# A hybrid attention / mLSTM / Hyena backbone: the late adaLN modulation computed by row sums on VectorE instead of matmuls

## The chip, the core and the metric

The kernel runs on one core of one Trainium2 chip. The metric is the device time of one execution in microseconds (us). The median of three runs of the kernel before is 3824.61 us (3822.61 to 3828.31).

## The reference, cut to what matters

Two layers (`DEPTH = 2`) work on 1024 latent tokens and 256 context tokens of width 1024. Each layer normalises its tokens, projects them, runs three groups of mixers side by side (latent attention with 8 heads, a chunked mLSTM, a Hyena convolution), projects back, and ends with a ConvFFN. Everything is modulated by six vectors per layer and stream:

```
for i in range(DEPTH):
    mod_x = jax.nn.silu(c) @ ada_w[i] + ada_b[i]        # ada_w[i]: 1024 x 6144
    mod_c = jax.nn.silu(c_ctx) @ ada_w[i] + ada_b[i]
    sh1, sc1, g1, sh2, sc2, g2 = jnp.split(mod_x[:, None, :], 6, axis=-1)
    csh1, csc1, cg1, csh2, csc2, cg2 = jnp.split(mod_c, 6, axis=-1)
    hx = rmsnorm(x, norm1_g[i]) * (1.0 + sc1) + sh1
    ...
    x = x + g1 * (jnp.concatenate([att_x, ml_x, hy_x], axis=-1) @ w_out[i])
    x = x + g2 * conv_ffn(rmsnorm(x, norm2_g[i]) * (1.0 + sc2) + sh2, ...)
```

So each of the two streams (latent and context) needs 6144 dot products of length 1024 per layer; in layer 1 the context stream needs only `csh1` and `csc1`, because its output is not used. The values depend on nothing but `c`, `c_ctx` and weights. `sh1` and `sc1` are needed at the start of a layer, `g1` at its output projection, `sh2` and `sc2` at its second norm, `g2` at the end of its FFN.

## The kernel before, in words

Features lie on the 128 partitions, tokens along the columns, in blocks of 512, 512 and 256 (context) columns. A float32 product is carried by three float32r matmuls (`mm3`) of hi and lo parts; a weight tile is loaded into `wr`, cast to hi on ScalarE (line 300) and its lo part is a subtraction on VectorE, or on GpSimd during the FFN (line 301).

The stages of a layer follow each other, layer 0 and then layer 1, and overlap at their ends:

- **mixers** (`mixers_in`): input projections on TensorE; `conv_tiles` makes a depthwise convolution along a row `raw` with one ScalarE and two VectorE instructions; `ml_states` and `ml_out` are the mLSTM, in which each chunk of 128 tokens makes a small tile `nd` on VectorE;
- **hyena** (`hyena`);
- **attention** (`attention`): units of one block of queries and one head. A unit of a latent block has ten steps, one per tile of 128 keys: three matmuls into a bank `st` (96 or 97 rows x 512), two exponentials on ScalarE (`P` and its rounded form `Ph`), `Pl = P - Ph` on VectorE in even steps and on GpSimd in odd steps (line 1344), three matmuls into `pv`. Between the steps, row maxima of the coming unit are taken: one matmul into a bank `sm` (two banks) and a VectorE reduction (line 1308). Layer 0 has 16 such units and 8 short ones for context queries; layer 1 has the 16 alone;
- **w_out** and the second norm, then **ffn**: 44 products (`begin`, `piece`) into one of two PSUM tiles `u3` of 1536 columns in layer 0, each followed by `conv` (one ScalarE and two VectorE passes over the tile), interleaved with the down projection in two banks `pj` and `pk`, whose results VectorE adds to the stream (line 1515).

The modulation is made by `ada`: four loads of 256 KB of `ada_w`, 8 matmuls with the 32-column stationary `cs` (silu of both conditions; the profile shows each of them as two), a ScalarE copy of the bank into `adarow`, 2 small matmuls that fold it, a VectorE addition into `mods`. One call makes 256 features of both streams. The first 8 calls (`sh1`, `sc1` of layer 0) run at the start. The other 40, that is 16 for layer 0 and 24 for layer 1, all run in the attention of layer 0, six after each pair of units, planned as if traced 300 instructions later (`after`, `LATER_A`); they use the bank `pk` and five blocks `ada_w` of the ring `B`.

The order on every engine is not written by hand: a planner (`schedule_with_timeline_sim=True`) simulates the program with its own costs and issues what is ready by priority, which is the order of tracing. Once planned it is fixed: each engine and each DMA queue works through its list in order and waits at the head of it. Nearly all loads are issued by one queue, SyncE's (SP).

Of the kernel before, what the change touches and what calls it, by code (L numbers as in the profile page):

```python
# [9 lines left out]
F32 = mybir.dt.float32  # L10
# [12 lines left out]
TP = 1282                     # token axis with a zero after each stream: x 0:1024, 0, ctx 1025:1281, 0  # L23
# [11 lines left out]
# (first token, columns, stream: 0 latent / 1 context)  # L35
# [16 lines left out]
def _consts():  # L52
# [47 lines left out]
def _host(inp):  # L100
    """Lay the inputs out for the chip: slices, transposes, replication."""
# [4 lines left out]
    def colmaj(a):                       # [L, n*128] -> [L, 128, n]  # L106
        return a.reshape(a.shape[0], -1, 128).transpose(0, 2, 1)
# [3 lines left out]
    o["adaw"] = g["ada_w"].reshape(L, 4, 2, 128, 12, 512).transpose(0, 4, 1, 3, 2, 5).reshape(L, 12, 4, 128, 1024)  # L111
# [48 lines left out]
    qk = np.zeros((L, 2, 2, 128, 128), np.float32)           # [L, pair, q/k, in, out]  # L160
# [9 lines left out]
    o["hyv"] = np.stack([g["hy_b1"], g["hy_b2"], g["hy_sin_freq"]], -1)   # [L,64,3]  # L170
# [12 lines left out]
NADA = 6  # L183
# [6 lines left out]
class Kern:  # L190
    def __init__(self, tc, a, out):
        self.tc, self.nc, self.a, self.out = tc, tc.nc, a, out
        self.n = self.turn = self.wturn = 0
        self.wx = None
# [48 lines left out]
    def later(self, by):  # L243
        """Scheduled as if traced `by` instructions later: work that fills gaps."""
# [9 lines left out]
    def mm3(self, out, lh, ll, rh, rl, start, stop):  # L254
        """One K tile of a float32 product carried by three float32r passes."""
# [1187 lines left out]
    def ffn(self, L, xs, hs, rp, pp, between):  # L1443
# [19 lines left out]
        def conv(u):  # L1463
# [6 lines left out]
            if ab == 0:  # L1470
                nc.scalar.activation(y[:, :W], y[:, :W], AF.Silu)
# [217 lines left out]
```

## Time and profile before

| | |
|---|---|
| median of three runs | 3824.61 us (3822.61 to 3828.31) |
| profiled execution: span from first to last instruction | 3828.4 us (no other time of it is given; the highest of the three runs is 3828.31) |
| TensorE matmul (PE) busy | 3547.6 us (93%), 17696 instructions |
| VectorE (DVE) busy | 2001.4 us (52%), 3037 instructions |
| ScalarE (ACT) busy | 1294.6 us (34%) |
| GpSimd (POOL) busy | 923.9 us (24%) |
| HBM read | 263.50 MB |

Busy time of PE is a model for overlapping matmuls: a busy PE need not run at its peak. PEld is its weight load, which overlaps. [...] SPq is the queue of SyncE, which issues DMAs. Stages by the trace: mixers of layer 0 from about 95 to 400 us, attention of layer 0 from about 584 (its first exponential) to 1046 us (the first result of the output projection), FFN of layer 0 to about 2100; mixers of layer 1 from about 2200 to 2489 and its attention from 2629 (table load of its exponentials) to 2976.

### The profile page before, as it was taken

To read this page: it belongs to the slowest core of one execution; us is meant where nothing else is said; L and a number is where in the kernel's file an instruction comes from. 1 tells how busy PE (TensorE), PEld (TensorE's weight loads), DVE (VectorE), ACT (ScalarE), POOL (GpSimd) and SP (SyncE) were. 2 spreads that over 40 slices of the span, in tenths; PEclk is the share of its full clock that TensorE was granted. 3 is DMA by queue.
4 is the path that set the end of the run, shared out by engine and by line. 5 is a ranking of instruction groups with operands and counts; after the bars stand their busy time and mean duration, and the time that the engine had idled before them with its cause. 6 is when DMAs were issued, how large, how long until landed. Compare 5 with 4: busy or idle time off the path is not lost.

```text
span 3828.4 us, 45926 instructions
## 1 busy us (share of the span) xinstructions
PE 3547.6 (93%) x17696; PEld 2809.5 (73%) x17696; DVE 2001.4 (52%) x3037; ACT 1294.6 (34%) x2108; POOL 923.9 (24%) x782
## 2 busy tenths in 40 slices
PE   5999869989899999999999799978999999999997
PEld 3798755556677888888888678856666778888885
DVE  5646675445565433434334765566666543444345
ACT  4433314445543221212112443324566432222222
POOL 1402442222311111111112141143334122222221
PEclk8999989989999999999999899889999999999998
DMA  5322544466242111111111222343232311111111
GB/s 176 115 69 90 198 130 141 126 168 170 71 138 66 39 34 39 39 33 34 39 39 39 94 95 88 108 141 105 54 84 80 102 44 44 45 55 45 44 50 66
DMA packets 195007, 319.46 MB, mean 83 GB/s; under 512 B 32207, under 2 KB 112160, under 8 KB 194788
## 3 DMA queue, kind: packets, MB, share of 16 engines
q1 hardware_dynamic: 194244, 316.23, 26.6%
q8 instruction: 139, 2.28, 0.3%
q14 instruction: 80, 0.66, 0.1%
q0 software_dynamic: 544, 0.31, 0.0%
HBM read 263.50 MB, written 52.81 MB: 83 GB/s over the span
## 4 chain that ended last, share of the span: by engine, by line
PE 59%; DVE 6%; DMA 3%; ACT 2%; issue 2%; POOL 1%; SPq 0%; DVEq 0%; ACTq 0%; POOLq 0%
PE u L252 29%; PE pk L252 12%; PE pj L252 12%; PE st L252 2%; PE pv L252 2%; PE hf L252 1%; ACT wh L300 1%; PE mi L252 0%; DVE B L456 0%; DMA vst<-Ph 0%; PE sm L252 0%; DVE sa L453 0%; PE mo L252 0%; DMA B<-mix 0%; DVE S L1515 0%
## 5 line engine op out<-in xcount | busy, mean ns | idle before, releaser
L252 PE MATMUL u<-B,wh 128*128 128x512 f32 (+1 forms) x3240 | 727.0, 376 | 17.6 <-ACT wh L300 10.6
L252 PEld LDWEIGHTS u<-B,wh 128*128 128x128 f32 x3240 | 573.9, 189 | 141.3 <-ACT wh L300 12.7
L301 POOL TENSOR_TENSOR wh<-wr,wh 128x1024 fp32r<-128x1024 f32 x92 | 222.3, 2416 | 1116.1 <-ACT wh L300 1116.1
L300 ACT CAST wh<-wr 128x1024 fp32r<-128x1024 f32 (+2 forms) x188 | 188.8, 1005 | 775.9 <-PE u L252 425.8
L252 PE MATMUL u<-B,wx 128*128 128x512 f32 (+1 forms) x2040 | 435.1, 367 | 2.3 <-DVE sa L1469 2.3
L252 PEld LDWEIGHTS u<-B,wx 128*128 128x128 f32 x2040 | 352.6, 189 | 70.9 <-issue 2.5
L252 PE MATMUL pj<-B,wh 128*128 128x512 f32 (+1 forms) x1644 | 381.8, 378 | 16.2 <-DVE wh L301 7.0
L252 PE MATMUL pk<-B,wh 128*128 128x512 f32 (+1 forms) x1485 | 355.9, 386 | 31.9 <-ACT S L588 7.8
L252 PEld LDWEIGHTS pj<-B,wh 128*128 128x128 f32 x1644 | 288.5, 193 | 83.6 <-issue 11.9
L252 PEld LDWEIGHTS pk<-B,wh 128*128 128x128 f32 x1485 | 265.7, 197 | 102.2 <-issue 15.3
L1515 DVE SCALAR_TENSOR_TENSOR S<-pk,mods,S 128x512 f32<-128x512 f32 (+1 forms) x220 | 152.7, 694 | 322.5 <-PE pk L252 322.3
L1344 POOL TENSOR_TENSOR Pl<-P,Ph 128x512 fp32r<-128x512 f32 (+1 forms) x168 | 219.4, 1306 | 405.9 <-ACT Ph L1343 349.1
L1515 DVE SCALAR_TENSOR_TENSOR S<-pj,mods,S 128x512 f32<-128x512 f32 (+1 forms) x220 | 152.7, 694 | 307.9 <-PE pj L252 307.8
L252 PE MATMUL st<-qh,S 96*128 96x512 f32 (+1 forms) x960 | 292.7, 411 | 15.1 <-DMA qh<-mr 7.9
L1308 DVE TENSOR_REDUCE mx<-sm 128x1 f32<-128x512 f32 (+1 forms) x400 | 227.6, 588 | 116.4 <-PE sm L252 114.1
L1468 DVE SCALAR_TENSOR_TENSOR sa<-u,ffc,sa 128x1281 f32<-128x1281 f32 (+1 forms) x88 | 124.3, 1413 | 276.3 <-ACT sa L1467 275.0
L1342 ACT ACTIVATE P<-st 128x512 f32<-128x512 f32 (+1 forms) x336 | 197.9, 590 | 162.0 <-PE st L252 82.4
L252 PE MATMUL pk<-g,wh 128*128 128x512 f32 (+1 forms) x1032 | 242.2, 370 | 7.7 <-ACT g L283 3.6
L252 PE MATMUL pj<-g,wh 128*128 128x512 f32 (+1 forms) x1032 | 245.1, 370 | 2.7 <-POOL wh L301 1.6
L252 PEld LDWEIGHTS st<-qh,S 96*128 96x128 f32 (+1 forms) x960 | 183.0, 196 | 75.0 <-DMA qh<-mr 12.2
L252 PE MATMUL pv<-Ph,B 128*64 128x512 f32 (+2 forms) x672 | 213.1, 398 | 12.7 <-ACT Ph L1343 8.4
L252 PEld LDWEIGHTS pk<-g,wh 128*128 128x128 f32 x1032 | 179.6, 189 | 43.8 <-DVE S L1515 4.2
(391 smaller groups left out, 5048.5 us busy)
## 6 DMA issues: line engine op xcount, KB each, us to landing
B<-in_adaw_dram SPq DMA_DIRECT2D x192, 256.0 KB
wr<-in_wup_dram SPq DMA_DIRECT2D x88, 512.0 KB
wr<-in_wdn_dram SPq DMA_DIRECT2D x50, 512.0 KB
wr<-in_wout_dram SPq DMA_DIRECT2D x40, 512.0 KB
wr<-in_win_dram SPq DMA_DIRECT2D x28, 512.0 KB
S<-in_xT_dram SPq DMA_DIRECT2D x16, 640.0 KB
mlrb<-rrows SPq DMA_DIRECT2D x36, 256.0 KB
B<-mix SPq DMA_DIRECT2D x32, 256.0 KB
```

Of the source, the lines that this page charges most:

```text
L252: self.nc.tensor.matmul(out, lhsT, rhs, start=start, stop=stop)
L300: self.nc.scalar.copy(hi, wr)
L301: (self.nc.gpsimd if self.wpool else self.nc.vector).tensor_tensor(lo, wr, hi, op=ALU.subtract)
L1308: nc.vector.reduce_max(st["mx"][:, qt, bi:bi + 1], ps[:, :kn], axis=AX.X)
L1342: nc.scalar.activation(P[:, :n], ps[:, :n], AF.Exp, scale=SCALE)
L1344: (nc.gpsimd if j % 2 else nc.vector).tensor_tensor(Pl[:, :n], P[:, :n], Ph[:, :n], op=ALU.subtract)
L1468: nc.vector.scalar_tensor_tensor(y[:, 1:W], pu[:, 0:W - 1], cw[:, 0:1], y[:, 1:W], op0=ALU.mult, op1=ALU.add)
L1515: nc.vector.scalar_tensor_tensor(x, ps, self.mods[L][:, 40 + m, s:s + 1], x, op0=ALU.mult, op1=ALU.add)
```

## The change

The 8 calls of `ada` at the start stay. The other 40 go, and the same features are made by VectorE alone. The host lays the rest of `ada_w` out transposed (`adawT`: 80 tiles of 128 features x 1024). Silu of both conditions is also made as two rows and kept in DRAM (`silu_rows`, `crow`); a stage loads pieces of them, repeated on all 128 partitions (`crows`). One `tensor_tensor_reduce` multiplies a piece of a weight tile (256 or 512 columns) by the row, sums along the columns, adds the bias or the sum so far, and writes one column of `mods`. It also has to write its products somewhere: they go over a tile that the stage has just finished with (`out`), which ties the instruction to its place.

`ada_rows` is a generator that issues the loads and the sums; a stage starts it (`ada_start`) and sends it such tiles (`ada_some(out, n)`: n sums). Where they are: after each convolution of the mixers (4, over `raw`) and each mLSTM chunk (4, over `nd`); in attention after the even steps of a unit (1, over `P`, in step 4 two); in the FFN of layer 0 after each convolution (3, over the PSUM tile `u3`).

| stage | features | columns | sums | loads, KB each |
|---|---|---|---|---|
| mixers 0 | 16 to 23 of layer 0, both streams | 256 | 64 | 32 x 128 |
| attention 0 | 24 to 47 of layer 0, both streams | 512 | 96 | 48 x 256 |
| FFN 0 | 0 to 15 of layer 1, both streams | 256 | 128 | 64 x 128 |
| mixers 1 | 16 to 31 of layer 1, latent | 256 | 64 | 64 x 128 |
| attention 1 | 32 to 47 of layer 1, latent | 512 | 32 | 32 x 256 |

(A feature here is a group of 128.) The counts follow from the calls below: groups x pieces of a row of 1024 x streams. The pool of `P` in attention goes from two buffers to three, in both layers; the weight tiles have their own buffers (`aw`: 3 or 4 in the mixers, 2 in attention, 3 in the FFN). The diff also removes comments, which are left out here.

```
...
+    def silu_rows(self, sp):
+        nc = self.nc
+        r = self.t(sp, [2, 1024], "crow")
+        nc.sync.dma_start(r, self.a["cb"])
+        nc.scalar.activation(r, r, AF.Silu)
+        nc.sync.dma_start(self.crow[:, :], r)
+
+    def crows(self, t, s, c0):
+        n = t.shape[-1]
+        self.nc.sync.dma_start(t, self.crow[s, c0:c0 + n].unsqueeze(0).to_broadcast([128, n]))
+        return t
+
+    def ada_rows(self, L, fs, streams, n, wt, rt):
+        nc = self.nc
+        for c0 in range(0, 1024, n):
+            rows = [(s, self.crows(rt(s, c0), s, c0)) for s in streams]
+            for f in fs:
+                w = wt()
+                nc.sync.dma_start(w, self.a["adawT"][f - 16 if L == 0 else 32 + f][:, c0:c0 + n])
+                for s, r in rows:
+                    out = yield
+                    m = self.mods[L][:, f, s:s + 1]
+                    nc.vector.tensor_tensor_reduce(out=out[:, :n], in0=w, in1=r, scale=1.0,
+                                                   scalar=m if c0 else self.adab[L][:, f, s:s + 1],
+                                                   op0=ALU.mult, op1=ALU.add, accum_out=m)
+
+    def ada_some(self, out, n=1):
+        try:
+            for _ in range(n):
+                if self.adas is not None:
+                    self.adas.send(out)
+        except StopIteration:
+            self.adas = None
...
+            self.ada_some(raw, 4)
             ys.append(y)
...
+            rm = self.pool(e, f"rm{L}", aw=4 if last else 3)
+            self.ada_start(L, range(16, 32) if last else range(16, 24), (0,) if last else (0, 1), 256,
+                           lambda: self.t(rm, [128, 256], "aw"),
+                           lambda s, c0: self.t(rm, [128, 256], f"ar{s}"))
...
+                self.ada_some(nd.rearrange("p a b c -> p (a b c)"), 4)
                 nc.gpsimd.tensor_tensor(hh[:, 0], hh[:, 0], hh[:, 1], op=ALU.add)
...
                 (nc.gpsimd if j % 2 else nc.vector).tensor_tensor(Pl[:, :n], P[:, :n], Ph[:, :n], op=ALU.subtract)
+                if j % 2 == 0:
+                    self.ada_some(P, 2 if j == 4 else 1)
...
-                after()
...
             nc.vector.scalar_tensor_tensor(y[:, 0:W - 1], pu[:, 1:W], cw[:, 2:3], y[:, 0:W - 1], op0=ALU.mult, op1=ALU.add)
+            self.ada_some(pu, 3)
...
+                self.silu_rows(rp)
                 for nb in range(4):
                     for half in range(2):
                         self.ada(0, nb, half, lambda: self.blk(dt=F32), pp, "a0")
...
-                todo = [(x, i, h) for x, a0 in ((0, 4), (1, 0)) for i in range(a0, 12) for h in range(2)] if L == 0 else []
-
-                def next_w():
-                    ada_w.append(ada_w.pop(0))
-                    return ada_w[-1]
-
-                def after():
-                    with self.later(LATER_A):
-                        for _ in range(NADA):
-                            if todo:
-                                self.ada(*todo.pop(0), next_w, self.pj, "pk")
...
-                    rp = self.pool(e3, f"r3{L}", P=2, Ph=3, Pl=3, cos=1, sin=1)
-                    rq = self.pool(e3, f"rt{L}", qh=8, qc=4, mx=3, nm=2, mr=2, num=2, dd=2, rb=1)
-                    if L == 0:
-                        ada_w = [self.blk((128, 512), F32) for _ in range(5)]
+                    rp = self.pool(e3, f"r3{L}", P=3, Ph=3, Pl=3, cos=1, sin=1)
+                    rq = self.pool(e3, f"rt{L}", qh=8, qc=4, mx=3, nm=2, mr=2, num=2, dd=2, rb=1, aw=2)
+                    streams = (0,) if last else (0, 1)
+                    rows = {(s, c0): self.blk(dt=F32) for s in streams for c0 in (0, 512)}
+                    self.ada_start(L, range(32 if last else 24, 48), streams, 512,
+                                   lambda: self.t(rq, [128, 512], "aw"), lambda s, c0: rows[s, c0])
...
+                    if not last:
+                        ar = [self.t(rp, [128, 256], "rs_d"), self.t(self.cp, [128, 256], "adarow")]
+                        self.ada_start(1, range(16), (0, 1), 256, lambda: self.t(rp, [128, 256], "aw"), lambda s, c0: ar[s])
                     self.ffn(L, xs, hs, rp, pp, between)
...
```

## Rows read from the trace of the kernel before

**Rows 1.** The page's slices: 40 equal parts of the span, busy share in tenths.

```profile
PE   5999869989899999999999799978999999999997
PEclk8999989989999999999999899889999999999998
```

**Rows 2.** The attention of layer 0 and of layer 1, busy time by engine.

```profile
core 0: us, PE busy (x) PEld busy (x) DVE busy (x) ACT busy (x) POOL busy (x), PEclk, DMA share, GB/s
584.00:1046.00 462.00, 412.52 (x2218) 277.56 (x2216) 228.74 (x465) 222.70 (x463) 135.21 (x128) 0.92 0.47 132
2629.00:2976.00 347.00, 326.56 (x1405) 230.25 (x1404) 220.77 (x387) 211.39 (x408) 135.13 (x110) 0.99 0.23 67
```

**Rows 3.** Layer 0's stretch again: line 365 alone, then tile adarow (with ACT).

```profile
584.00:1046.00 462.00, 54.47 (x608) 19.11 (x608) 0.92 0.47 132
...
584.00:1046.00 462.00, 19.68 (x152) 22.97 (x152) 14.23 (x38) 0.92 0.47 132
```

**Rows 4.** Waits in that stretch: us in total, times, longest.

```profile
PE pk L365 <- DMA B<-in_adaw_dram: 25.7, 10, 5.8
```

**Rows 5.** Waits in the attention of layer 1, 2629 to 2976 us.

```profile
ACT P L1342 <- POOL Pl L1344: 25.8, 20, 3.4
...
PEld sm L252 <- DVE mx L1308: 6.1, 11, 1.7
...
PEld sm L252 <- DVE mr L1316: 1.9, 4, 0.6
...
PEld pk L252 <- DVE P L1205: 1.2, 1, 1.2
```

**Rows 6.** VectorE groups by form, whole run: count, busy us, mean ns, idle before.

```profile
L1344 DVE TENSOR_TENSOR Pl<-P,Ph 128x512 fp32r<-128x512 f32 x160 | 130.9, 818 | 119.7 <-ACT Ph L1343 106.6 <-PE pv L252 6.1 <-PE st L252 2.6
...
L875 DVE TENSOR_TENSOR mlX<-mlX,ms 128x512 f32<-128x512 f32 x36 | 23.0, 677 | 4.9 <-PE ms L252 4.9
...
L453 DVE SCALAR_TENSOR_TENSOR ntmp<-S,A,nrb 128x512 f32<-128x512 f32 x16 | 11.2, 740 | 0.0
...
L456 DVE SCALAR_TENSOR_TENSOR B<-sa,mods,B 128x256 fp32r<-128x256 f32 x16 | 7.5, 481 | 1.6 <-ACT B L455 1.6
```

**Rows 7.** Two VectorE lines: ns min/median/max, first and last start, forms.

```profile
L453 DVE SCALAR_TENSOR_TENSOR sa<-S,A,g x64: 476/744/2781, 1118.8 to 3076.1; 128x512 f32<-128x512 f32 x48, 128x256 f32<-128x256 f32 x16
...
L373 DVE TENSOR_TENSOR mods<-pk,adab x40: 133/160/164, 570.5 to 981.5; 128x4 f32<-128x4 f32 x40
```

**Rows 8.** Mixers of layers 0 and 1, then FFN of layer 0.

```profile
95.00:400.00 305.00, 299.53 (x1962) 258.44 (x1961) 184.30 (x333) 113.50 (x208) 86.33 (x104) 0.99 0.28 91
2201.00:2489.00 288.00, 277.09 (x1686) 235.04 (x1685) 174.94 (x323) 103.42 (x184) 71.96 (x91) 0.95 0.30 97
1150.00:2100.00 950.00, 933.67 (x4745) 787.91 (x4744) 391.05 (x427) 203.58 (x186) 158.56 (x66) 1.00 0.12 39
```

**Rows 9.** TensorE's waits, mixers 0 (95 to 400), then FFN 0 (1244 to 2100).

```profile
PEld mo L252 <- DVE kw L820: 1.2, 1, 1.2
...
PE u L252 <- ACT wh L300: 10.6, 10, 1.1
```

**Rows 10.** SyncE's queue in the FFN of layer 0, 1244 to 2100: its waits.

```profile
SPq L288 <- POOL wh L301: 432.7, 29, 27.7
SPq L1501 <- POOL wh L301: 183.9, 10, 27.7
SPq L288 <- POOL wx L301: 121.7, 9, 13.6
SPq L1501 <- POOL wx L301: 49.3, 11, 13.5
```

**Rows 11.** DMA issues, whole run.

```profile
B<-in_adaw_dram SPq DMA_DIRECT2D x192, 256.0 KB
```

**Rows 12.** The start, in order of time: start us, us, engine, line.

```profile
20.38 22.75 SPq L360 DMA_DIRECT2D B<-in_adaw_dram  x32
...
19.76 1.28 ACT L316 ACT_TABLE_LOAD   x1
21.06 0.22 ACT L316 ACTIVATE c_cs<-c_cT 128x16 f32<-128x16 f32 x1
```

More of the change, by code (lines that the diff above doesn't have):

```diff
@@ L110, in _host @@
     o["cT"] = np.stack([g["c"][0], g["c_ctx"]], -1).reshape(8, 128, 2).transpose(1, 0, 2)
-    o["adaw"] = g["ada_w"].reshape(L, 4, 2, 128, 12, 512).transpose(0, 4, 1, 3, 2, 5).reshape(L, 12, 4, 128, 1024)
+    o["adaw"] = g["ada_w"][0, :, :2048].reshape(4, 2, 128, 4, 512).transpose(3, 0, 2, 1, 4).reshape(4, 4, 128, 1024)
+    aT = g["ada_w"].transpose(0, 2, 1).reshape(L, 48, 128, 1024)
+    o["adawT"] = np.concatenate([aT[0, 16:], aT[1]], 0)
+    o["cb"] = np.stack([g["c"][0], g["c_ctx"]])
     o["adab"] = np.repeat(colmaj(g["ada_b"])[..., None], 2, -1)
@@ L180, in _host @@
     return {k: np.ascontiguousarray(v, np.float32) for k, v in o.items()}
-NADA = 6
 LATER_A = 300
@@ L193, in __init__ @@
         self.n = self.turn = self.wturn = 0
-        self.wx = None
+        self.wx = self.adas = None
         self.wpool = False
@@ L359, in ada @@
             w = wt().rearrange("p (k c) -> p k c", k=2)
-            nc.sync.dma_start(w, self.a["adaw"][L, nb, kp].rearrange("p (k c) -> p k c", k=2)[:, :, 256 * half:256 * half + 256])
+            nc.sync.dma_start(w, self.a["adaw"][nb, kp].rearrange("p (k c) -> p k c", k=2)[:, :, 256 * half:256 * half + 256])
             ws.append(w)
@@ L373, in ada, with gain, ada_start @@
         nc.vector.tensor_tensor(self.mods[L][:, sl, :], pm, self.adab[L][:, sl, :], op=ALU.add)
-        if half and nb in (3, 9):
-            A, sc, g = ((self.A1, 8, 0) if nb == 3 else (self.A2, 32, 1))
-            nc.vector.scalar_tensor_tensor(A[L], self.mods[L][:, sc:sc + 8, :], 1.0, self.ng[L][:, g],
-                                           op0=ALU.add, op1=ALU.mult)
+        if half and nb == 3:
+            self.gain(L, 0)
+    def gain(self, L, i, ns=2):
+        A, sc = ((self.A1, 8), (self.A2, 32))[i]
+        self.nc.vector.scalar_tensor_tensor(A[L][:, :, :ns], self.mods[L][:, sc:sc + 8, :ns], 1.0,
+                                            self.ng[L][:, i, :, :ns], op0=ALU.add, op1=ALU.mult)
+    def silu_rows(self, sp):
[21 more added lines that the diff above has]
+                                                   op0=ALU.mult, op1=ALU.add, accum_out=m)
+    def ada_start(self, *args):
+        self.adas = self.ada_rows(*args)
+        next(self.adas)
+    def ada_some(self, out, n=1):
[5 more added lines that the diff above has]
+            self.adas = None
     def inv_rms(self, acc, n, dim, sp, ps):
@@ L700, in mixers_in @@
                         nc.sync.dma_start(self.hyx[i][:, 1024:1280], y[:, 1025:1281])
+            assert self.adas is None
         with ExitStack() as e:
@@ L1155, in proj, with attention @@
             self.mm3(out, wh[:, o:o + 128], wl[:, o:o + 128], hi, lo, k == 0, k == m - 1)
-    def attention(self, L, after):
+    def attention(self, L):
         nc, a = self.nc, self.a
@@ L1532, in ffn @@
         accs = {}
+        assert self.adas is None
+        if not last:
+            self.gain(L + 1, 0)
         self.wpool = WP
@@ L1578, in run @@
                 ))
+            self.crow = dt_("crow", [2, 1024])
             self.xsp = [dt_(f"xsp{i}", [128, NX]) for i in range(8)]
@@ L1593, in run @@
             with ExitStack() as e0:
-                rp = self.pool(e0, "r0", nacc=1, nsq=1, ntmp=4, nrb=2, rs_s=2, rs_r=2, rs_v=2, rs_d=1)
+                rp = self.pool(e0, "r0", crow=1, nacc=1, nsq=1, ntmp=4, nrb=2, rs_s=2, rs_r=2, rs_v=2, rs_d=1)
                 pp = self.pool(e0, "p0", PSUM, a0=6)
+                self.silu_rows(rp)
                 for nb in range(4):
@@ L1606, in run @@
                 self.mixers_in(L)
-                todo = [(x, i, h) for x, a0 in ((0, 4), (1, 0)) for i in range(a0, 12) for h in range(2)] if L == 0 else []
-                def next_w():
-                    ada_w.append(ada_w.pop(0))
-                    return ada_w[-1]
-                def after():
-                    with self.later(LATER_A):
-                        for _ in range(NADA):
-                            if todo:
-                                self.ada(*todo.pop(0), next_w, self.pj, "pk")
-                att = self.attention(L, after)
+                att = self.attention(L)
                 with ExitStack() as e2:
@@ L1632, in run @@
                         pass
+                    assert self.adas is None
+                    self.gain(L, 1, len(streams))
                 with ExitStack() as e4:
-                    rp = self.pool(e4, f"r5{L}", sa=2, g=6, wx=2, rs_s=1, rs_r=1, rs_v=1, rs_d=1)
+                    rp = self.pool(e4, f"r5{L}", sa=2, g=6, wx=2, aw=3, rs_s=1, rs_r=1, rs_v=1, rs_d=1)
                     src = a["xT"] if L == 0 else self.xsp
@@ L1669, in run @@
                     self.wpool = True
+                    if not last:
+                        ar = [self.t(rp, [128, 256], "rs_d"), self.t(self.cp, [128, 256], "adarow")]
+                        self.ada_start(1, range(16), (0, 1), 256, lambda: self.t(rp, [128, 256], "aw"), lambda s, c0: ar[s])
                     self.ffn(L, xs, hs, rp, pp, between)
```

## The prediction

> **What bounds the kernel now.** I read the page's slices first: TensorE is at nine tenths nearly everywhere, at full clock over the long flat part, which is the FFN of layer 0, and the thinner digits lie at the start, around the Hyena stage and in the attention of layer 0 [rows 1]. The reader should see that the kernel is bound by TensorE, so that matmul time removed where TensorE sets the pace is time gained.
>
> Then I set the two attention stretches side by side, from the first exponential to the first result of the output projection in layer 0, and from the exponentials' table load to the end of the last unit in layer 1 [rows 2]. They do the same 16 units; layer 0 has 8 short context units and all 40 calls of `ada` besides. [...] Then I asked for the instructions of `ada` alone [rows 3] and for TensorE's waits on their loads [rows 4].
>
> **What goes.** In the stretch of layer 0, `ada` holds TensorE for 54.5 us in its products and 19.7 us in its folds, which are 608 + 152 instructions [rows 3]; the products wait another 25.7 us for their weights [rows 4]. Together 99.9 us. A second way to the same: without these, 2218 - 608 - 152 = 1458 matmuls are left, and at the pace of layer 1 (347 us for 1405) they take 360 us, which is 102 less than 462 [rows 2]. So I put the removal at 100 us. The second way carries layer 1's better clock with it. Of the waits and of the modelled busy time some may have been cover for something else, so the lower bound is the matmul time halved, 37 us; a rival below rests on that. The 38 small additions into `mods` leave VectorE too: 38 x 0.16 = 6 us [rows 7].
>
> **What a sum costs.** No `tensor_tensor_reduce` is in the trace. The nearest rows are two-input VectorE instructions over SBUF: 0.74 us for 512 columns, 0.48 us for 256 [rows 6], so 0.26 us for each 256 columns more. With GpSimd at work beside it the subtraction `Pl` takes 0.82 us in the mean, where a like one with its second input in PSUM takes 0.68 [rows 6], and one instruction of line 453 took 2.78 us [rows 7]: two SBUF inputs collide with GpSimd. In attention I take 0.74 + (0.82 - 0.68) = 0.88 us. Below, 0.68; above, a sum at half pace, 0.74 + 2 x 0.26 = 1.26 us, and 0.74 us for 256 columns.
>
> [...]
>
> **What the sums do, stage by stage.**
>
> *Attention, layer 0.* 96 x 0.88 = 84 us on VectorE. It stands at 229 - 6 = 223 us; with the sums 307 of 362 us, 85%, up from 50%. Behind a sum on VectorE queue the maxima, which empty the two `sm` banks, and the next `Pl`; TensorE waits for the first, and for the second through `pv`. In layer 1, where VectorE is 221/347 = 64% busy, TensorE's waits on it come to 6.1 + 1.9 + 1.2 = 9.2 us [rows 5]. I let such waits grow as busy share over idle share, an estimate: 0.85/0.15 against 0.64/0.36 is 3.2 times. So 9.2 x 362/347 = 9.6 us become 31: **+21**. Nothing (sums only in idle time) and all 84 us are the ends. The loads, 256 KB each [rows 11], fall from 152 to 48; they pass the same queue as the small transfers at the end of each unit, which gains them room. `Pl` on GpSimd collides with more; GpSimd is busy for 29% of the stretch, so I count it at nothing, and at one collision of 0.14 us each, 13 us, if that cover is gone.
>
> *Attention, layer 1.* Six sums a unit, so 32 are done in 5.3 of 16 units, some 116 us, with 28 us of sums on 74: 88% busy. Its share of the waits, 3.1 us, grows by 0.88/0.12 over 1.78 = 4.1 times: **+10**; all 28 us at most. The third `P` buffer meets ScalarE's wait for GpSimd's `Pl`, 25.8 us here [rows 5]. TensorE need not follow, so I take nothing, and up to 10 us at the good end.
>
> *Mixers.* 64 x 0.5 = 32 us on VectorE in each layer: 184 becomes 216 of 305 us (71%), 175 becomes 207 of 288 (72%) [rows 8]. TensorE is full at 299.5 of 305 us, and its largest wait on VectorE there is 1.2 us [rows 9]; that cover hides the sums. The delay to the next chunk of the mLSTM is on VectorE itself, and the input projections fill TensorE meanwhile. **+5** for both layers, for sums that sit in front of a weight's lo part; 64 us if the cover is gone.
>
> *FFN, layer 0.* 128 sums of 0.5 us and, with GpSimd busy for 17% and a collision costing up to 2.78 - 0.74 = 2 us, some 0.7: 90 us. VectorE goes from 391 to 481 of 950 us, 51% [rows 8]. The PSUM tile is kept some 2 us longer; 44 products over 950 us leave 21.6 us each and there are two tiles, so the next but one waits on the convolution long before it must. TensorE's listed wait here is for ScalarE's cast, 10.6 us [rows 9]. **+4**.
>
> *Start.* One more Silu, at most one more table load of 1.28 us [rows 12], a load and a store ahead of or between the 32 weight loads that take 22.75 us to issue: **+3**. Row pieces (2 in attention 1, 4 in attention 0, 8 in the FFN, 8 and 4 in the mixers) are 26 short loads, issued a stage's pass ahead; nothing.
>
> **The sum**: -100 + 21 + 10 + 5 + 4 + 3 = **-57 us**. On the profiled execution's 3828.4 us that is 3771; it stands 3.8 us above the median of the runs, so for the median 3824.6 - 57 = **3768 us**.
>
> **The rivals.**
>
> 1. *The sums cost nothing.* VectorE's waits in attention are for TensorE and ScalarE, and sums could sit in these. Then -100 + 3, and up to -110 with the third `P`: 3715 to 3740, say 3725. Against it: 85% busy leaves few gaps of 0.88 us.
>
> 2. *The sums run at half pace.* 1.26 + 0.14 = 1.40 us in attention: 134 us on 223 is 357 of 362 us. VectorE becomes the bound of that stage; filled to 90% it takes 397 us, which leaves 65 of the 100. Layer 1: 74 + 45 = 119, at 90% 132 against 116, +16. Mixers +10, FFN +8, start +3: -28, 3797 us. [...]
>
> 3. *Slower: sums wait for their loads in the FFN.* SyncE's queue works in order, and in the FFN it stands at its head waiting for a weight buffer for 433 + 184 + 122 + 49 = 788 of 856 us, in 59 waits of 13 us, at most 27.7 [rows 10]. The 64 new loads have to be issued among these. One that is planned behind a weight load which in truth waits longer arrives late; the sum stops VectorE, the convolution and the down results stop behind it, and TensorE has two banks to go on with. 16 loads late by half a wait, 6.6 us, cost 106 us: 3768 + 106 = 3874. It decides from 57 us on, nine such. Against it: sums come 21.6 us apart in groups of three and three buffers are filled a group ahead, and the like loads in attention held TensorE up by 5.8 us at worst [rows 4].
>
> 4. *No change: the matmuls of `ada` were gap fillers.* They are planned late on purpose. If only 43 us come back, the 43 of the additions eat them: 3825 us. Against it: layer 1 has no such fillers and its TensorE is at 94% all the same.
>
> **How the numbers follow.** Chances: forecast (3750 to 3795) 0.52, rival 1 0.14, rival 2 0.14, rival 3 0.13, rival 4 0.07. A change of 0.2%, 7.6 us, is about what a measurement of this kernel can tell from none. Faster: the first three less the slow edge of rival 2, 0.79; same: rival 4 and that edge, 0.08; slower 0.13. The range takes in rivals 1, 2 and 4 and stops short of the edge below (the third `P` with all else free) and of rival 3: 3718 to 3828 us.
>
> **What would show it.** Attention of layer 0 in 375 to 395 us with a clock near 0.98 and VectorE at 80 to 85%; a sum at 0.8 to 0.95 us in attention and about 0.5 in the mixers; attention of layer 1 some 10 us longer; FFN and mixers within 5 us of before. A sum of 1.3 us or more is rival 2; TensorE at or below 0.97 in the FFN, with VectorE waiting there for `aw` loads, is rival 3. I am wrong above all if VectorE's queue holds TensorE up more than the busy share tells, since each stage's order is planned anew.

## The result: 1.2% slower, and the profile after

The changed kernel takes 3870.53 us (3869.14 to 3872.51, 4 runs) beside 3823.61 us for the kernel before on the same chip: ratio 1.0122, 95% interval 1.0108 to 1.0136. The forecast was 3768 us, the range 3718 to 3828. The profiled execution is 3869.14 us, its span 3867.3.

The page's slices of the changed kernel (they answer to [rows 1]; PEclk is the granted clock of TensorE, here in tenths of its full speed):

```profile
PE   5998978888988999999998898678999999999997
...
PEclk8998988898999999999999998889999999999998
```

A slice is some 97 us here. Attention of layer 0, slices 7 to 11, is shorter but no denser: eights stand there where there were nines. The loss shows in the mixers: slice 4 (290 to 387 us, layer 0) falls from nine to eight, slices 25 and 26 (2320 to 2514 us, layer 1) from nine to eight and six.

To see which stage gave and which took, I marked each one by rows of single tiles: the mixers of layer 0 end with the first copy into `hA`, attention runs from the first exponential into `P` to the last copy into `num`, the FFN from its first to its last convolution on `sa<-u`; what follows up to the next `hA` is the FFN's tail and the mixers of layer 1. The changed kernel's rows (duration in ns as min/median/max, then first and last start in us), up to the `hA` of layer 1:

```profile
L1051 ACT COPY hA<-hf x8: 372/479/587, 480.7 to 524.4; 128x512 f32<-128x512 f32 x4, 128x256 f32<-128x256 f32 x4
L1399 ACT ACTIVATE P<-st x176: 376/598/631, 611.1 to 1044.3; 128x512 f32<-128x512 f32 x160, 128x256 f32<-128x256 f32 x16
L1413 ACT COPY num<-pv x24: 359/582/585, 628.7 to 1051.7; 65x512 f32<-65x512 f32 x16, 65x256 f32<-65x256 f32 x8
L1525 ACT ACTIVATE sa<-u,ffc x44: 1413/1420/1427, 1182.3 to 2073.6; 128x1282 f32<-128x1282 f32 x44
L1051 ACT COPY hA<-hf x8: 372/488/592, 2534.7 to 2560.2; 128x512 f32<-128x512 f32 x4, 128x256 f32<-128x256 f32 x4
```

So its stages last 480.7, 1051.7 - 611.1 = 440.6, 2073.6 - 1182.3 = 891.3 and 2534.7 - 2073.6 = 461.1 us. The same marks in every kernel of this study, in us (the rest of a span is 1207 to 1225 us, and 1240 in e3; times are medians, with the 95% interval of the ratio to the kernel before; the stages are those of one profiled execution each, which for e6 took 13 us more than its median):

| kernel | to the end of mixers 0 | attention 0 | FFN 0 | tail and mixers 1 | attention 1 | time | ratio |
|---|---|---|---|---|---|---|---|
| before | 451.6 | 504.4 | 885.2 | 418.5 | 353.1 | 3823.61 | |
| changed | 480.7 | 440.6 | 891.3 | 461.1 | 375.1 | 3870.53 | 1.0108 to 1.0136 |
| e1_raw_free | 490.2 | 436.4 | 891.7 | 453.0 | 372.3 | 3868.79 | 1.0098 to 1.0134 |
| e2_nd_free | 464.5 | 438.7 | 892.2 | 428.8 | 370.4 | 3821.22 | 0.9990 to 1.0011 |
| e3_att_dump | 481.2 | 452.5 | 892.9 | 456.4 | 369.7 | 3891.76 | 1.0162 to 1.0193 |
| e4_att_aw | 478.6 | 439.1 | 892.0 | 459.0 | 370.3 | 3863.30 | 1.0089 to 1.0120 |
| e5_no_sums | 450.2 | 418.9 | 886.3 | 419.4 | 357.2 | 3745.90 | 0.9780 to 0.9814 |
| e6_both_free | 477.1 | 453.1 | 892.0 | 434.7 | 378.5 | 3840.39 | 1.0029 to 1.0065 |
| e7_att1_thin | 482.8 | 443.5 | 892.1 | 460.4 | 373.7 | 3865.47 | 1.0086 to 1.0124 |
| e8_ffn_all | 472.0 | 451.2 | 895.0 | 416.2 | 368.1 | 3817.75 | 0.9965 to 0.9989 |
| e9_hy_only | 461.1 | 444.1 | 895.1 | 415.3 | 359.9 | 3792.59 | 0.9894 to 0.9927 |
| e10_att_all | 451.9 | 472.1 | 895.9 | 417.1 | 358.4 | 3814.10 | 0.9957 to 0.9978 |
| e12_p2 | 472.6 | 448.5 | 894.7 | 415.9 | 354.5 | 3812.06 | 0.9948 to 0.9974 |
| e13_hy_both | 456.7 | 453.4 | 891.5 | 422.5 | 373.0 | 3820.41 | 0.9978 to 0.9999 |
| e14_best | 457.2 | 445.6 | 894.5 | 415.1 | 349.6 | 3789.91 | 0.9893 to 0.9927 |
| e15_after_p2 | 482.0 | 444.6 | 892.1 | 460.2 | 367.1 | 3867.66 | 1.0092 to 1.0122 |

The first two lines hold the result: attention of layer 0 gives 64 us, the mixers take 29 + 43, attention of layer 1 takes 22 and the FFN 6. The attention and the FFN of layer 0 do what was forecast, more or less. The mixers do not.

Windows of the changed kernel: mixers 0, mixers 1 from the mLSTM on, attention 0, attention 1, FFN 0 (columns as in [rows 2]; they answer to [rows 2, 8]):

```profile
95.00:481.00 386.00, 360.84 (x2206) 306.10 (x2205) 241.84 (x516) 135.16 (x257) 100.48 (x118) 0.94 0.35 112
2279.00:2535.00 256.00, 205.43 (x1197) 170.11 (x1196) 142.11 (x332) 73.22 (x151) 44.63 (x54) 0.85 0.35 113
611.00:1052.00 441.00, 398.48 (x1644) 283.18 (x1643) 340.41 (x647) 234.71 (x469) 158.74 (x131) 0.90 0.33 93
2648.00:3023.00 375.00, 351.21 (x1450) 247.25 (x1449) 256.78 (x452) 214.01 (x408) 136.99 (x111) 0.95 0.30 88
1182.00:2074.00 892.00, 872.81 (x4473) 739.74 (x4472) 418.44 (x622) 179.70 (x151) 149.34 (x63) 1.00 0.15 47
```

In the mixers of layer 1 VectorE is busy for only 142 of 256 us, 56%, and no engine is full: TensorE's work of 205 us leaves it idle for 51. In the kernel before, the like stretch took 214 us:

```profile
2303.00:2517.00 214.00, 200.60 (x1196) 170.05 (x1195) 115.86 (x219) 72.45 (x151) 42.55 (x54) 0.90 0.31 99
```

VectorE's busy share can't be the explanation. In the mixers of layer 0, the stretch 340 to 380 us shows the same, and TensorE's granted clock there is 0.87 where the kernel before had 1.00 and a TensorE busy for all 40 us (the kernel before, then the changed one):

```profile
340.00:380.00 40.00, 40.00 (x229) 34.71 (x228) 13.69 (x14) 12.72 (x25) 5.34 (x9) 1.00 0.27 89
```

```profile
340.00:380.00 40.00, 30.95 (x165) 26.03 (x163) 25.04 (x57) 14.09 (x30) 6.45 (x6) 0.87 0.25 73
```

What VectorE does there, in order of time, in one chunk of the mLSTM (start us, duration us):

```profile
318.70 0.69 DVE L952 TENSOR_TENSOR mlhh<-mlnd,mlden 128x512 f32<-128x512 f32 x1
...
319.92 0.96 DVE L412 CUSTOM_DVE_ANT_0 mlnd<-aw,ar,mods 128x256 f32<-128x256 f32 x1
...
321.15 0.47 DVE L412 CUSTOM_DVE_ANT_0 mlnd<-aw,ar,mods 128x256 f32<-128x256 f32 x1
...
321.66 0.48 DVE L412 CUSTOM_DVE_ANT_0 mlnd<-aw,ar,mods 128x256 f32<-128x256 f32 x1
...
322.41 0.47 DVE L412 CUSTOM_DVE_ANT_0 mlnd<-aw,ar,mods 128x256 f32<-128x256 f32 x1
...
322.99 0.43 DVE L941 TENSOR_TENSOR mlnd<-mi,mlE 128x260 f32<-128x260 f32 x1
```

`mlhh` is the last reader of the chunk's `nd` (one buffer). Its four sums, which write over `nd`, follow, and only then may the next chunk write `nd` (line 941). The tie puts the four sums between every two chunks. VectorE waits little for their weights: 1.8 us for `aw` in all the sums of mixers 0, and 9.1 us in mixers 1 from the mLSTM on.

How far this stretches the chunks can be read from the starts of `mlhh`. They come in two halves, five and five in layer 0 (four and four in layer 1), with a pause between. Chunks 1, 5, 6 and 10 of layer 0, first without any sums (e5, below), then in the changed kernel:

```profile
291.81 0.69 DVE L952 TENSOR_TENSOR mlhh<-mlnd,mlden 128x512 f32<-128x512 f32 x1
...
328.94 0.69 DVE L952 TENSOR_TENSOR mlhh<-mlnd,mlden 128x512 f32<-128x512 f32 x1
...
381.33 0.69 DVE L952 TENSOR_TENSOR mlhh<-mlnd,mlden 128x512 f32<-128x512 f32 x1
...
411.29 0.69 DVE L952 TENSOR_TENSOR mlhh<-mlnd,mlden 128x512 f32<-128x512 f32 x1
```

```profile
292.77 0.69 DVE L952 TENSOR_TENSOR mlhh<-mlnd,mlden 128x512 f32<-128x512 f32 x1
...
346.28 0.69 DVE L952 TENSOR_TENSOR mlhh<-mlnd,mlden 128x512 f32<-128x512 f32 x1
...
373.24 1.40 DVE L952 TENSOR_TENSOR mlhh<-mlnd,mlden 128x512 f32<-128x512 f32 x1
...
413.61 0.69 DVE L952 TENSOR_TENSOR mlhh<-mlnd,mlden 128x512 f32<-128x512 f32 x1
```

The same for both layers, in us, with three kernels from below (layer 0 / layer 1; the first column counts from the start of the span, or from the end of FFN 0):

| kernel | to the first chunk | first half | pause | second half | from there to `hA` |
|---|---|---|---|---|---|
| e5, no sums | 291.8 / 282.3 | 37.1 / 34.3 | 52.4 / 44.8 | 30.0 / 21.4 | 38.9 / 36.6 |
| changed | 292.8 / 283.6 | 53.5 / 39.6 | 27.0 / 27.4 | 40.4 / 44.9 | 67.1 / 65.7 |
| e1 | 291.3 / 282.6 | 55.2 / 43.7 | 56.8 / 37.9 | 34.6 / 27.9 | 52.4 / 60.9 |
| e2 | 305.3 / 299.9 | 38.8 / 34.8 | 54.1 / 43.7 | 31.7 / 18.1 | 34.6 / 32.3 |
| e13 | 292.9 / 290.1 | 43.7 / 42.6 | 59.1 / 40.6 | 27.9 / 19.0 | 33.0 / 30.3 |

The two halves together grow by 27 us in layer 0 and by 29 in layer 1. The last chunk of layer 0 comes hardly later (413.6 against 411.3 us), but only because the pause is shorter, and the pause is the time that Hyena projections fill: without sums seven of their results go into a row between 341 and 389 us, in the changed kernel none. They come later: the last Hyena convolution starts at 436.8 us instead of 398.3, behind the last chunk.

### The profile page after: what moved, and what is told of

Its sections match the earlier page's. It is cut to its first block, busy times and chain, and to the rows that moved or that the text cites. A ratio compares the mean times of both kernels' runs of the same rounds, so it can differ in the third digit from the quotient of the medians.

```text
span 3867.3 us, 45515 instructions
## 1 busy us (share of the span) xinstructions
PE 3525.5 (91%) x16896; PEld 2803.5 (72%) x16896; DVE 2247.4 (58%) x3765; ACT 1285.9 (33%) x2069; POOL 939.3 (24%) x782
## 4 chain that ended last, share of the span: by engine, by line
PE 61%; DVE 9%; DMA 4%; issue 3%; ACT 2%; POOL 1%; SPq 0%; DVEq 0%; ACTq 0%; POOLq 0%
PE u L255 29%; PE pj L255 11%; PE pk L255 11%; PE st L255 3%; PE pv L255 3%; DMA aw<-in_adawT_dram 1%; PE sm L255 1%; DVE mx L1365 1%; ACT wh L303 1%; PE hf L255 1%; DVE wh L304 1%; DVE P L412 0%; DVE B L506 0%; DMA vst<-Ph 0%; DVE sa L503 0%
## 5 line engine op out<-in xcount | busy, mean ns | idle before, releaser
L1401 POOL TENSOR_TENSOR Pl<-P,Ph 128x512 fp32r<-128x512 f32 (+1 forms) x168 | 232.6, 1385 | 380.9 <-ACT Ph L1400 313.2
L255 PE MATMUL st<-qh,S 96*128 96x512 f32 (+1 forms) x960 | 302.7, 424 | 24.4 <-DMA qh<-mr 20.8
L1574 DVE SCALAR_TENSOR_TENSOR S<-pk,mods,S 128x512 f32<-128x512 f32 (+1 forms) x220 | 152.6, 694 | 291.3 <-PE pk L255 291.2
L255 PEld LDWEIGHTS st<-qh,S 96*128 96x128 f32 (+1 forms) x960 | 191.8, 206 | 86.0 <-DMA qh<-mr 26.7
L255 PEld LDWEIGHTS pk<-g,wh 128*128 128x128 f32 x1032 | 179.8, 189 | 43.7 <-ACT g L286 4.0
```

Of the source, the lines that this page charges most:

```text
L255: self.nc.tensor.matmul(out, lhsT, rhs, start=start, stop=stop)
L1401: (nc.gpsimd if j % 2 else nc.vector).tensor_tensor(Pl[:, :n], P[:, :n], Ph[:, :n], op=ALU.subtract)
L1574: nc.vector.scalar_tensor_tensor(x, ps, self.mods[L][:, 40 + m, s:s + 1], x, op0=ALU.mult, op1=ALU.add)
```

## The experiments

I had three theories at first. A: the sums tied to the Hyena rows come last in tracing order and hold the row buffers, which starves the Hyena projections that fill TensorE beside the mLSTM. A': the sums between the chunks lengthen the mLSTM's chain. B and C for attention: too few weight buffers, or the tie to `P`; against both, D: VectorE has too much to do.

**e1_raw_free and e2_nd_free** cut one tie each (the changed lines alone):

```
# e1: convolutions
-            self.ada_some(raw, 4)
+            self.ada_some(self.dump, 4)        # adarow, 128 x 256, unused there
# e2: mLSTM chunks
-                self.ada_some(nd.rearrange("p a b c -> p (a b c)"), 4)
+                self.ada_some(self.dump, 4)
```

> The sums after the convolutions of the mixers write their products over a constant tile of 256 columns that nothing else uses there, and no longer over the convolution's input row; their number and order stay, and those of the mLSTM chunks still write over their own tile. Theory A (rows held: the sums tied to the Hyena rows come last in the tracing order, so five and more of the eight row buffers stay held until the mLSTM's output is done, and the Hyena projections that fill TensorE beside it can't start): the mixers of layer 0, from the first store of the mLSTM rows to the first tile of the Hyena stage, go back from 265 to some 240 us, those of layer 1 lose some 35 of the 41 us they gained, and the kernel takes some 3812 us. Rival A' (four sums in each mLSTM chunk make VectorE's chain there longer, whoever holds rows): nothing moves, 3865 to 3875.

> The other half of the same cut: the sums of the mLSTM chunks write over the constant tile instead of the chunk's own small tile, of which there is one buffer, and those of the convolutions still write over the row. Theory A: nothing moves, 3865 to 3875. Rival A' in the form that the chunk's tile is held too long: the next chunk starts before the four sums of the one before, and up to 4 x 0.57 us for each of 18 chunks, 41 us, come back: 3830. In the form that the sums are simply on VectorE's list, nothing moves either; then the first kernel decides.

Theory A falls as the cause: with the rows free the kernel takes 3868.79, 2 us less than the changed one. Freeing `nd` alone brings 49 us back, 3821.22: 16 in mixers 0 and 32 in mixers 1. The rows do hold the Hyena projections up: with the rows free they fill the pause again (56.8 us, and 37.9 in layer 1). But the halves of the mLSTM stay long, so letting the rows go early only moves the loss. TensorE and then ScalarE at the end of its mixers 0 (in brackets the idle time before and its releaser):

```profile
446.57 0.69 PE L973 MATMUL mm<-c_ident,hb 128*128 128x128 f32 x2 [13.20 <-DVE hb L970]
...
455.95 8.13 PE L256 MATMUL pj<-B,wh 128*128 128x512 f32 x24 [2.80 <-ACT sq L643]
```

```profile
455.30 0.60 ACT L643 ACTIVATE sq<-pj 128x512 f32<-128x512 f32 x1 [1.38 <-DVE mods L413]
```

The Hyena projections were used up as filler early, the second half of the mLSTM ran with little beside it, and the transposes waited 13.2 us for `hb`, while VectorE went through the last chunks and eleven sums. Then the square (`sq`) of the next projection waited for the last sum, at 455, though it reads none of them; I take it that its pool reuses the memory of their weight tiles. In the changed kernel's layer 1 the same place costs more: TensorE waits 17.3 us for that square, and the square starts at 2499.2, just as the last sum ends (the wait there is listed under a load from `hyx`).

**e3_att_dump and e4_att_aw** take the tie, or the small number of weight buffers, from attention:

```
# e3
+                    self.dump = self.blk(dt=F32)
-                    self.ada_some(P, 2 if j == 4 else 1)
+                    self.ada_some(self.dump, 2 if j == 4 else 1)
# e4: aw in turns over the two old buffers and 1 (layer 0) or 3 (layer 1) blocks of the ring B
```

> In attention the sums write over a block of their own and no longer over the tile of exponentials P. Theory C (the tie: the next exponential waits for the sum, which waits for its weights): ScalarE's waits for the sums, 21 us in layer 0 and 10 us in layer 1, go, and attention gets shorter by 10 to 25 us in all: 3845 to 3860. Theory D (VectorE has too much to do there): nothing moves beyond 5 us, 3866 to 3875.

> In attention the weight tiles of the sums get three buffers in layer 0 and five in layer 1, where there were two; the sums write over P as in the changed kernel. Theory B (with two buffers the next weight load stands at the head of SyncE's queue until a sum is through, and the small transfers at the end of each unit stand behind it): the queue's waits on sums, 64 us in layer 0 and 29 in layer 1, fall to a third in layer 1 and by less in layer 0; TensorE's waits for the row of maxima, 12.6 and 7.9 us, fall with them, and attention of layer 1 gets shorter by 8 to 15 us: 3850 to 3862. Theory D: nothing moves beyond 5 us.

In both, attention of layer 1 gets 5 us shorter, and that of layer 0 12 us longer (e3) or 1.5 us shorter (e4). e3 loses another 18 us ahead of attention 1, between `hA` and the first exponential (131.8 against 113.5), where nothing was edited but a block of the ring taken. Neither takes attention of layer 1 clearly below the 370.4 to 378.5 us of five kernels in which nothing differs there (changed, e1, e2, e6, e13). e3 tests C: ScalarE's waits for sums are gone and the gain is 5 us of the 22, so C falls as the main cause. e4 doesn't test B, because its edit didn't take the wait away. SyncE's queue stands as long at the loads of layer 1 with five buffers (second line) as with two:

```profile
SPq L408 <- DVE mods L412: 29.0, 20, 7.0
```

```profile
SPq L409 <- DVE mods L413: 28.2, 15, 6.8
```

In e3 these waits halve, to 14.0 us, and attention of layer 1 is 5 us shorter. So B stays open.

**e5_no_sums** leaves the sums out:

```
-        self.adas = self.ada_rows(*args)
-        next(self.adas)
+        pass                                    # and the vectors are set to a constant
```

> The matmuls of the late modulation are gone as in the changed kernel, and the sums, their weight loads and the row pieces too: the late modulation vectors are left out of the computation (they hold a constant), all else stays. This prices the removal by itself. The prediction's first term (100 us) gives 3825 to 3730 us, with 65 to 70 us of it in attention of layer 0 and its sums then worth the rest; the mixers, the FFN and attention of layer 1 are as before, within 5 us each. Rival (the third buffer for P and the new planning alone make attention of layer 1 and the mixers longer): these stages keep 10 us or more of their 17 to 42 us, and the kernel takes 3760 us or more.

It takes 3745.90: the removal alone is worth 80 us, and the sums cost 3870.5 - 3745.9 = 125 us. By stage, changed minus e5: mixers 30.5 + 41.7, attention 21.7 and 17.9, FFN 5.0, and 11 in the stretches between, which no run assigns to a cause (128 by the profiled spans). The rival, that the third `P` or the new planning is to blame, falls for the mixers and keeps 4 us in attention 1.

**e6_both_free** joins e1 and e2.

> Both halves of the cut in the mixers together: no sum there writes over a row or over a chunk's tile, all write over one constant tile. Theory now (the sums between two chunks of the mLSTM are what costs: the chunk's tile has one buffer and its four sums have to run, and their weights to land, before the next chunk may write it): as with the chunk's tile alone, 3815 to 3827. If the held rows also cost something once the chunks are free: some 10 us less, 3805 to 3815.

Neither: it takes 3840.39, 19 more than e2 alone. In e2 the sums that nothing ties were planned early, into the serial chain of the mLSTM's gates, ahead of its output. VectorE in e2:

```profile
205.14 0.28 DVE L805 TENSOR_TENSOR mlB<-mlB 64x128 f32<-64x128 f32 x1
205.45 0.29 DVE L806 TENSOR_TENSOR mlB<-mlB 64x128 f32<-64x128 f32 x1
205.77 0.48 DVE L413 CUSTOM_DVE_ANT_0 adarow<-aw,ar,mods 128x256 f32<-128x256 f32 x1
...
206.18 0.28 DVE L805 TENSOR_TENSOR mlB<-mlB 64x128 f32<-64x128 f32 x1
206.49 0.29 DVE L806 TENSOR_TENSOR mlB<-mlB 64x128 f32<-64x128 f32 x1
206.81 0.48 DVE L413 CUSTOM_DVE_ANT_0 adarow<-aw,ar,mods 128x256 f32<-128x256 f32 x1
```

A step of that scan, two instructions of line 805 and 806, takes 1.04 us with a sum and 0.63 without. The first product of the mLSTM's output (`mlnd<-mi`) starts at 292.1 us in e2 and at 279.8 in e5. In e6, where none is tied, the first `mlhh` comes at 316.9 us, after 305.3 in e2 and 291.8 in e5.

**e7_att1_thin** spreads the sums of attention 1 over all its units (`j in (2, 6)` there instead of every even step).

> In attention of layer 1 the 32 sums stand two to a unit over all 16 units, where they stood six to a unit in the first five and a third. Theory D (VectorE too full in that first third, 86 per cent busy): the 22 us that attention of layer 1 gained fall to 5 to 12, and the kernel takes 3855 to 3862 us. Rival (each sum or each weight load costs its piece wherever it stands, 0.7 us a sum): it stays at 20 to 24, 3868 to 3873.

373.7 against 375.1 us: the price stays when the 32 sums are spread over all 16 units, so D in the form of a too full first third falls.

**e8_ffn_all** moves all of layer 1's sums to the FFN of layer 0, **e9_hy_only** and **e10_att_all** move the 64 sums of layer 0's mixers as well, **e12_p2** takes e8 with two buffers for `P` in layer 1 (cut to the sums; e9 is shown against e8):

```
# e8: FFN 0 makes features 0 to 15 of layer 1 for both streams, then 16 to 47 for the latent one
-            self.ada_some(pu, 3)
+            self.ada_some(pu, 6)
# e9, in conv_tiles; no sums between the mLSTM's chunks
-            self.ada_some(self.dump, 4)
+            if tiles[0][0][0] == "H":           # the six Hyena convolutions
+                self.ada_some(raw, 11)
# e10: none in the mixers; attention 0 makes features 16 to 47
-                    self.ada_some(P, 2 if j == 4 else 1)
+                    self.ada_some(P, 2 if j in (0, 4, 8) else 1)
```

> All sums of layer 1 stand in the FFN of layer 0, six after each of its convolutions where there were three (256 sums of 256 columns instead of 128); the mixers and the attention of layer 1 have none. The mixers of layer 0 write over the constant tile. If the FFN's sums cost what its first 128 did, 6 us, its second 128 cost 6 to 10; the mixers of layer 1 and its attention go back to before, -10 and -17 against the kernel with the chunk's tile free: 3795 to 3808, faster than the kernel before. If VectorE's queue becomes the FFN's bound or its loads come late, the FFN of layer 0 gains 30 us or more and the kernel takes 3825 or more.

> As the kernel with all of layer 1's sums in the FFN of layer 0, but the 64 sums in the mixers of layer 0 stand after the six Hyena convolutions alone, eleven each, over the convolution's row; none stands after the mLSTM's convolutions or between its chunks. Theory (sums cost where they stand in a serial chain on VectorE: between the chunks of the mLSTM, 29 us, or, when nothing ties them, ahead of it in the chain of its gates, 13 to 22 us; a Hyena convolution is in no such chain): the mLSTM's first chunk is back at 281 us where it had moved to 302, the mixers of layer 0 take 450 to 460 us to the first tile of the Hyena stage where they had 472, and the kernel takes 3798 to 3808. Rival (64 sums cost the mixers 13 us or more wherever they stand, as VectorE's time or by the queue of their loads): 3815 to 3830.

> As the kernel with all of layer 1's sums in the FFN of layer 0, but the mixers of layer 0 have no sums either: their features are made in attention of layer 0, as 32 more sums of 512 columns beside the 96 there, eight to a unit instead of six. The mixers of layer 0 go back to 450 to 453 us. If what a sum costs in that attention stays at 22 us / 96 = 0.23 us each, attention gets 7 us longer than the 441 to 451 us of the kernels with 96: 3800 to 3808. If VectorE is the bound there (341 us busy of 441, and 28 more), all 28 us and the waits behind it come on top: 3818 to 3830.

> As the kernel with all of layer 1's sums in the FFN of layer 0, with two buffers for P in layer 1's attention where there were three; no sums stand there in either. That attention took 368 us without sums and 353 in the kernel before. Theory (the third buffer makes the planner's order there worse): back to 350 to 357, and 3803 to 3810 in all. Rival (two plans of the same work differ by that much for no single reason): 360 or more, 3812 to 3822.

e8 came in 10 us above its faster bracket, with the stages of layer 1 as expected but for attention (368 us with no sum in it) and the mixers of layer 0 at 472. e9 and e10 say where that stood: with the 64 sums behind the Hyena convolutions the mixers end at 461, with none at 452. e9 beat its bracket, 3792.59. e10 went the other way: 32 more sums made attention 0 21 us longer (472.1 against 451.2), three times the 7 us expected of them at the price of the first 96; the kernel, 3814.10, lies between its two brackets. VectorE is busy for 371 of 472 us there, so that it begins to bound the stage is likely, but not shown. In e12 attention 1 is back at 354.5, as the third buffer's theory said, while the kernel's 3812.06 lies at the edge of the rival's bracket. But e5, e8, e9 and e10 do the same work there with three buffers and take 357, 368, 360 and 358, so a plan's luck of some 10 us lies on top.

**e13_hy_both, e14_best, e15_after_p2.** e13 is the changed kernel with the mixers' sums of both layers behind the Hyena convolutions, eleven each; e14 is e9 with two `P` buffers in layer 1; e15 is the changed kernel with these.

> The changed kernel with one thing moved: in the mixers of both layers the 64 sums stand after the six Hyena convolutions alone, eleven each, over the convolution's row, and none between the chunks of the mLSTM or after its convolutions. The sums of attention and FFN stay as they are. Theory (the 70 us of the mixers come from the sums in the mLSTM's serial chain): the mixers lose 45 to 65 of them, 3805 to 3825 us. Rival (that the kernel with layer 1's sums in the FFN is fast comes from layer 1, and the place within the mixers matters only with one layer's sums): the mixers of layer 1, with 64 weight loads instead of 32, keep 20 us or more, 3835 to 3860.

> The fastest so far (layer 1's sums in the FFN of layer 0, layer 0's mixers with sums after the Hyena convolutions alone) with two buffers for P in layer 1's attention instead of three. If the two buffers are worth there what they were beside the other placement, attention of layer 1 goes from 360 to 354: 3785 to 3789. If that was the luck of one plan: 3790 to 3800.

> The changed kernel with two buffers for P in layer 1's attention, its 32 sums in place over P. If the third buffer is what made that attention longer (22 us), it goes from 375 to 360 or less: 3850 to 3858. If the sums did, two buffers make it worse, since a sum now holds one of two: 376 to 390, 3870 to 3885.

e13 settles the mixers. Same sums, same loads, same columns, another place (all tied to rows, none to `nd`): 456.7 and 422.5 us, 6.5 and 3.1 above e5, and the kernel goes from 3870.53 to 3820.41. The windows of its mixers 0, and of mixers 1 from the mLSTM on:

```profile
95.00:457.00 362.00, 347.94 (x2202) 295.87 (x2201) 237.23 (x516) 133.56 (x255) 101.55 (x118) 0.97 0.37 119
2271.00:2488.00 217.00, 196.83 (x1191) 165.52 (x1192) 143.97 (x344) 72.22 (x151) 45.27 (x54) 0.94 0.43 136
```

VectorE is as busy as in the changed kernel, 237 and 144 us, in stages 24 and 39 us shorter. The queue of the loads is an obvious rival. In the mixers of layer 1 it stands at the sums' weights for 53 us in e13 and 60 in the changed kernel, which is 39 us longer, so it doesn't carry the loss there; in those of layer 0 it is 43 and 61 us, and a part is not excluded.

e15 puts attention 1 at 367.1 with sums and two buffers, between its two brackets and 13 to 18 us above the 354.5 and 349.6 of e12 and e14 without sums. So both theories seem to have a part in its 22 us: the sums 13 to 18 (17.9 with three buffers, against e5), the third buffer the rest; in three pairs of kernels two buffers are better by 8 (changed, e15), 14 (e8, e12) and 10 us (e9, e14). A new plan alone moved this stage by up to 11 us, so the split is an estimate. e14 is the fastest version, 3789.91, 0.9% below the kernel before (e9 lies within its spread).

## Why the prediction was wrong

**The step that failed: mixers, +5, measured +72** (30.5 + 41.7). It read the cover from the wrong engine. "TensorE is full ... that cover hides the sums" is true of a sum in a gap, and the next sentence named the danger itself (the delay to the next chunk is on VectorE) and let the projections pay for it. But the projections are a fixed amount of filler: [rows 8] shows a TensorE full at 299.5 of 305 us, and what the chain beside it gains in length is lost again. The halves of the mLSTM gained 27 and 29 us, some 56 of the 72. In layer 1 the pause and the rest behind the last chunk together gained another 12 us; there TensorE stood 17.3 us for a square that started as the last sum ended. I counted 64 sums and 32 us of VectorE per layer. I didn't ask between which instructions they stand, though the change says so: the tie to `nd`, of which there is one buffer. The bad end written down, 64 us if the cover is gone, was near by luck: it is VectorE's time for the sums, and e13 spends that too, for 10 us. The range left it out.

**The removal: -100, measured -80** for the whole kernel, 85.5 of it in attention 0 (e5). By the marks of the prediction, from the first exponential to the first result of the output projection, e5 takes 374 us where the kernel before took 462: -89. The second way to the 100 carried layer 1's clock of 0.99 with it; in e5 attention 0 runs at 0.94. Where the other us went is open. TensorE's waits for the row of maxima on SyncE's queue are 10.5 us there and were 7.2 before, which explains 3.

**Price of a sum.** VectorE's rows for the sums in attention, in the mLSTM and in the FFN (ns, min/median/max):

```profile
L412 DVE DVE_READ_ACCUMULATOR2_ANT mods<- x384: 71/83/145, 175.8 to 2766.9; 128x1 f32 x192
...
L412 DVE CUSTOM_DVE_ANT_0 P<-aw,B,adab x64: 730/752/1880, 613.6 to 2702.4; 128x512 f32<-128x512 f32 x64
L412 DVE CUSTOM_DVE_ANT_0 P<-aw,B,mods x64: 730/752/2949, 818.1 to 2765.2; 128x512 f32<-128x512 f32 x64
...
L412 DVE CUSTOM_DVE_ANT_0 u<-aw,adarow,mods x48: 476/494/1664, 1396.2 to 2051.9; 128x256 f32<-128x256 f32 x48
```

0.75 and 0.49 us for an undisturbed one are the neighbours' 0.74 and 0.48 [rows 6], so rival 2 is out. Half pace, the upper bound of the prediction (1.26 us for 512 columns, 0.74 for 256), is shown by no run: the medians above are 0.75 and 0.49. With the long ones, up to 2.95 us, a sum in attention took 1.05 us in the mean (69.8 + 64.6 us for 128), plus 0.1 for the accumulator's read: 1.15 where I took 0.88. Beside the long ones GpSimd was at work, as the prediction had it: all 55 of the 128 that took over 0.76 us overlap an instruction of GpSimd, as do 39 shorter ones, and the 34 that overlap none took 0.73 to 0.75 us. No run sets the two apart with all else the same.

**Attention 0, +21: measured 21.7** (440.6 against e5's 418.9). The size was right, in part by luck. The scaling by busy over idle share has no great claim to it, since it stood on too low a price, and in eleven kernels with the same 96 sums this stage takes 436 to 453 us, 18 to 35 more than e5. By the prediction's marks it takes 396 us, where 375 to 395 was forecast; in the window above VectorE is at 77% and the clock at 0.90, where 80 to 85% and 0.98 was forecast.

**Attention 1, +10: measured 13 to 18**, undersized; that it doesn't fall with density (e7) says that the busy share was the wrong measure there. Which wait carries it stays open: SyncE's queue stood 29 us at loads for the sums and ScalarE 10.5 us behind them; without the latter (e3) attention is 5 us shorter, within the spread of plans, and no run took the former away whole. The third `P`, which I had put at nothing or a gain of up to 10 us, seems to have cost time.

**FFN, +4: measured 5.0. Start, +3:** nothing; the mLSTM's rows are stored at 215.3 us, as before (215.5). **Rival 3** ended near the measured time, 3874, for a reason that did not come: in the FFN of e14, with twice the loads, SyncE's queue waits 202.5 us for sums, and VectorE's longest wait for a weight is 2.6 us, 23 us in all.

```profile
SPq L409 <- DVE mods L413: 202.5, 167, 4.9
```

```profile
DVE u L413 <- DMA aw<-in_adawT_dram: 23.0, 22, 2.6
```

## What to carry to other kernels

Work spread into an idle engine is priced by the place, not by the engine's busy share: a sum that holds VectorE for some 0.6 us cost 0.04 us of time in the FFN (5.0 / 128), 0.05 to 0.17 behind a Hyena convolution (3.1 / 64 in layer 1 of e13, 6.5 to 10.9 / 64 in layer 0 of e13, e14 and e9), and 0.56 where most stood between the chunks of the mLSTM (72 / 128). Before placing it, list the serial chains that pass through that engine, and look at what a scratch output ties it to: a single-buffered tile puts it into the chain, and without a tie the planner here put it into another. Put it where a long regular stage has slack, even a whole layer early.

## What the runs showed that I had not expected

The same work, replanned, moved a stage with no edit in it: attention 1 without sums and with three `P` buffers by 11 us (357.2, 368.1, 359.9, 358.4), attention 0 with its 96 sums by 17 (436.4 in e1 to 453.4 in e13). A smaller difference in one of these stages says nothing by itself. The FFN of layer 0 is steadier: with its 128 sums it takes 891.3 to 892.9 us in nine kernels. And a TensorE left idle for a quarter of 40 us in the mixers also ran at a mean granted clock of 0.87 there (1.00 from 348 to 356 us, 0.50 from 358 to 366), so part of the wait may have been paid twice; what lowered the clock no run shows.
